# DeltaNet stage of a one-core layer: another interleaving of steps, inverses and dense units

## The chip, the core and the metric

The kernel runs on one core of a Trainium2 chip. A core has five engines with a queue of instructions each: PE (TensorE, matrix products into PSUM), DVE (VectorE), ACT (ScalarE), POOL (GpSimd) and SP (SyncE, here only for transfers). Each engine takes its instructions in order, and semaphores make one wait for another. DMA transfers are issued from the queues of SP, ACT and POOL. The metric is the device time of one execution in microseconds (us).

## The reference, cut to what matters

One layer over 640 tokens (128 of context, 512 latent), 1024 wide, in float32. The input is normalised and modulated, and projected to queries, keys and values of an attention branch, to those of a gated DeltaNet branch, and to gates. The outputs of both branches are projected, gated, added and projected again; a feed-forward part follows. The change touches the DeltaNet branch and what runs beside it:

```python
def _gated_delta_chunked(q, k, v, g, beta, s0):      # chunks of 64 tokens, 8 heads of 64
    ...
    a_mat = jnp.where(strict, einsum('nbhid,nbhjd->nbhij', kbeta, kb) * decay, 0.0) + jnp.eye(CHUNK)
    sol = lax.linalg.triangular_solve(a_mat, rhs, left_side=True, lower=True, unit_diagonal=True)
    qk = einsum('nbhid,nbhjd->nbhij', qb, kb) * decay
    def step(S, xs):
        v_new = uc - einsum('bhck,bhkv->bhcv', wc, S)
        o = einsum('bhck,bhkv->bhcv', qc * exp(gcc), S) + einsum('bhij,bhjv->bhiv', qkc, v_new)
        S = S * exp(glast) + einsum('bhck,bhcv->bhkv', kc * exp(glast - gcc), v_new)
        return S, o
```

It runs once forward and once backward over the tokens; for each direction the context gives a state of its own, and the latent tokens start from a given state. The chunks of one direction depend on each other through S.

## The kernel before, in words

The kernel goes through these stages: normalising and modulating the input; the DeltaNet projections and their convolution; the DeltaNet stage, in which the other projections ("dense units") run beside the recurrence; the attention; the merge; the feed-forward part. The change is in the DeltaNet stage, with small edits ahead of it and behind it.

**Dense units.** `dense(kinds)` walks over a string of letters and yields after each unit. `v`: the values of the attention, 5 units of 24 matmuls; `q`: a block of its queries or keys, 2 units of 24; `g`: a block of gates, 2 units of 24; `m` and `a`: a column block of the modulation weights, 1 unit of 16 matmuls, with a few more behind the next unit. The list that runs beside the recurrence is `FILL[1] = "vqmqmqmqmqmqmqmgmgagagagagagagaggagggggg"`: 67 units, with an `m` or an `a` after each pair of `q` or `g` for most of its length. A unit's weights are loaded raw on SP's queue into one of two buffers (`load_raw`, tag `raw`), and split into two float32r parts, `whi` by ACT (line 177) and `wlo` by DVE (line 178); three products (lines 197 to 199) make up one float32 product. `m` and `a` use raw weights (line 226). The result goes through ACT into a buffer of tag `gth` (three of them, shared with the rows of `m` and `a` and with the small gate tiles `gbn`) and is stored to DRAM on SP's queue (lines 879, 892, 904).

**Inverses.** `prep(mf, mb, buf)` prepares a pair of token tiles, one for each direction, in the order of `PAIRS` (five pairs, two steps of 64 tokens in each). It is a generator; its parts are: loads of decay logarithms into `rls` on POOL's queue (638, 639) and of stored gram matrices; three decay tiles (matmuls 603, 604 into the PSUM tile `ps_tb`, then an exp on ACT, 606) with the gram matrices (623) and their products `U` and `KQD`; then a substitution of 15 rounds on DVE (687 to 690) and a transpose `Zp` (698); then four small products, each depending on the one before by way of ACT or DVE: line 706 to `Gm` (ACT, 709), line 714 to `Yp` and `Zq` (DVE, 716 and 718), line 726 to `Gm` (731), lines 737 and 739 to `YZ` (748, 749). Lines 706 and 714 are 128 matmuls each.

**Steps.** `step` is a generator of three parts: (0) matmuls of the keys and queries with the state S (783), `kS` and `r` on DVE (786, 787); (1) `YZ` times `r` (793), then `vd` and `vn` on DVE (796, 798), `qS` and the scaled state on ACT (802, 808), and for a tile's second visit the load of the earlier output and its sum with `qS` on POOL (814); (2) `vd` into the new state (822, added on DVE at 825) and `vn` into the output (834). The right-hand side `r` is loaded on POOL's queue one step ahead (760). After a second visit `finish_o` normalises the output: a square on ACT (850, tile `fz`), a sum on DVE (852), a Newton iteration, a product on POOL (860) with a z tile loaded on ACT's queue (859), and four slots later a transpose on PE (598) and a store to `od_d` (868).

**The order.** PE's instructions stand in the order in which the program writes them (`manual_schedule`). The program is written in *slots*: `slot(*parts)` writes the next part of each generator given, then a part of each open `finish_o`, then one dense unit. The other engines' order comes from a planner that takes what is ready by its model, highest priority first; the priority says in how many slots a part is due. So between two parts in neighbouring slots lies one dense unit on PE. Before the change a step's parts stand in neighbouring slots, and so do the inverse's last four parts: 14 slots ahead of the first step, then for each pair the three slots of each of its two steps (two for the very first), one slot with a part of the inverse after next, four with the last four parts of the next inverse (the first two of which hold parts of the inverse after next as well), and five slots at the end. That is 67 slots.

The attention stage starts with loads of `qk_d` on ACT's queue (1057), rotations on DVE and POOL (1059 to 1070) and score matmuls (1084). Its filler on PE are the products of the merge's DeltaNet half, which read `od_d` (1156, 1157). `issue_after(ins)` puts the instructions that a block writes for the engine of `ins` behind `ins` in that engine's order; it adds nothing on other engines.

Of the kernel before, what the change touches and what calls it, by code (L numbers as in the profile page):

```python
# [18 lines left out]
P = 128  # L19
# [78 lines left out]
def body(ctx: ExitStack, tc: tile.TileContext, I, O, dbg=None):  # L98
# [64 lines left out]
    rawp = [None, 0]  # L163

    def load_raw(src, pool=None, tag="raw"):
# [108 lines left out]
    xa = tk.tile([P, 5, 512], F32, tag="xa", name="xa")  # L274
# [30 lines left out]
    with tc.tile_pool(name="xp", bufs=1, side="right") as xp:  # L305
# [4 lines left out]
        xTs = [y.rearrange("p t c -> p (t c)").rearrange("p (k c) -> p k c", k=4) for y in (xa, kt)]  # L310
        xT = [y[:, k] for y in xTs for k in range(4)]
        rawp[:] = [xp, 6]
        with tc.manual_schedule(engines={mybir.EngineType.SP}):
# [4 lines left out]
            for a, b in ((0, 2), (2, 4), (4, 5)):  # L318
# [8 lines left out]
                for t in range(a, b):  # L327
                    for i in range(2):
                        V.tensor_scalar(xh[i][:, t], xh[i][:, t], rr[:, t - a : t - a + 1], None, op0=ALU.mult)
                        ps = ps_t3()  # L330
                        for q in range(4):
                            PE.transpose(ps[:, q * 128 : q * 128 + 128], xh[i][:, t, q * 128 : q * 128 + 128], ident)
                        (S.copy if i == 0 else V.tensor_copy)(xTs[i][:, :, t * 128 : t * 128 + 128], ps.rearrange("p (k c) -> p k c", k=4))
# [142 lines left out]
    rls = tk.tile([P, 2, 640], F32R, tag="xa", name="rls")  # L476
# [102 lines left out]

    YZb = [[dn.tile([P, 512], F32, tag=f"YZ{d}{i}", name=f"YZ{d}{i}") for i in range(2)] for d in range(2)]  # L580
# [50 lines left out]
    def prep(mf, mb, buf):  # L631
# [13 lines left out]
        for d, m in ((0, mf), (1, mb)):  # L645
# [23 lines left out]
            kq = dn.tile([P, 512], F32, tag="KQD", name=f"KQD{d}", bufs=4)  # L669
# [31 lines left out]
        pg_ = ps_st(0)  # L701
# [9 lines left out]
        pc_ = ps_st(2)  # L711
# [9 lines left out]
        pg2 = ps_st(0)  # L721
# [11 lines left out]
        pc2 = ps_st(1)  # L733
# [7 lines left out]
        YZ = [YZb[d][buf] for d in range(2)]  # L741
# [8 lines left out]
        prs.append(dict(YZ=YZ, KQD=KQD, m=(mf, mb)))  # L750
# [12 lines left out]
    def step(si, pr, r, st, first, last=False):  # L763


        m = pr["m"]
# [9 lines left out]
        if St is not None:  # L776
# [10 lines left out]
            hold[:] = [V.tensor_tensor(r, r, kS, op=ALU.subtract).ins]  # L787
            yield
        pv = ps_st(1)
# [57 lines left out]
    def finish_o(ot, hv, rq, rq2):  # L847

        fz = dn.tile([P, 512], F32, tag="fz", name="fz")
# [21 lines left out]
    def fill_v(c):  # L871
        w = load_tok(I["w_v"][c], 256)
        cs = slice(c * 256, c * 256 + 256)
        for t in range(5):
# [4 lines left out]
            nc.sync.dma_start(v_d[t, :, cs], vv[:, :256])  # L879
            if t == 0:  # L880
                nc.sync.dma_start(O["vc"][:, cs], vv[:, :256])
            yield

    def fill_qk(i):
        hp, mi = i // 2, i % 2
        whi, wlo = load_w(I["w_qk"][i], KT, 128)
        for half in range(2):
# [4 lines left out]
            nc.sync.dma_start(qk_d[hp, mi, :, half * 320 : half * 320 + 320], vv)  # L892
            if mi == 1 and half == 0:
                nc.sync.dma_start(O["kc"][hp], vv[:, 0:128])
            yield

    def fill_gate(j):
        whi, wlo = load_w(I["w_gate"][j], KT, 128)
        for half in range(2):
# [4 lines left out]
            nc.sync.dma_start(gt_d[j, :, half * 320 : half * 320 + 320], th)  # L904
# [28 lines left out]
    hold = []  # L933
# [15 lines left out]
    with tc.manual_schedule(engines={mybir.EngineType.PE}):  # L949
# [13 lines left out]
        preps = [prep(*PAIRS[n], n % 2) for n in range(5)]  # L963
# [11 lines left out]
        for n in range(5):  # L975
            P1, P2 = [preps[i] if i < 5 else iter(()) for i in (n + 1, n + 2)]
            ahead(5, P2)
# [17 lines left out]
            if n < 3:  # L995
                slot((1, P2))
            if n < 4:
                for i in range(4):
                    slot((1, P1), *([((1, 8)[i], P2)] if i < 2 else []))
            if n == 3:  # L1000
                dpx.close()
        for _ in range(5):
# [20 lines left out]
    with (  # L1023
# [596 lines left out]
```

## Time and profile before

| | |
|---|---|
| median of 3 runs | 1173.38 us (1173.02 to 1174.58) |
| profiled execution | 1170.73 us, its span 1168.9 us |
| PE busy over the span | 1083.1 us (93%) |
| DVE, ACT, POOL busy | 861.3, 523.7, 342.3 us |
| granted clock, mean | 0.970 |

The span runs from the first to the last instruction; the time of an execution is a little longer. Busy time of PE counts matmuls in flight, so a busy PE isn't one at its peak. The granted clock is the share of its full rate that PE was given. Waits are put down to what ended last before the waiting instruction ran; "issue" is time for which the profile shows no cause. A DMA or a wait of a queue's sequencer has a q behind the engine's name.

### The profile page before, as it was taken

The numbers are of one execution on the slowest core, as the hardware profiler recorded it, in microseconds if no ns is written. First come the engines' busy times: TensorE is split into PE (matmuls) and PEld (weight loads), VectorE is DVE, ScalarE is ACT, GpSimd is POOL, SyncE is SP. The second block draws the span as 40 slices with busy tenths as digits, with TensorE's granted clock in tenths as the row PEclk, the third lists the DMA queues.
The fourth block names the chain that finished last, engine by engine and source line by source line (L and its number), as shares of the span: only waits on it lengthen the run. The fifth ranks groups of instructions, "written<-read, shape, count | busy, mean of one in ns | idle before, by whom it ended". The sixth has DMA issues, their size and how long they took to land.

```text
span 1168.9 us, 25017 instructions
## 1 busy us (share of the span) xinstructions
PE 1083.1 (93%) x10016; PEld 959.6 (82%) x10016; DVE 861.3 (74%) x1676; ACT 523.7 (45%) x1133; POOL 342.3 (29%) x277
## 2 busy tenths in 40 slices
PE   4999999989898988978999999979999999999996
PEld 3779999888787777876777899978979898897975
DVE  6567896884758486564755767887897989889785
ACT  5436343535453533424435353545544444444532
POOL 1343312101000001321221415544453544435213
PEclk9999999999999998987999999989999999999999
DMA  8831015656654534734333662066654565665515
GB/s 304 311 120 45 22 38 189 227 185 172 206 174 143 172 124 130 217 118 135 95 112 106 218 253 91 36 175 159 181 153 129 143 164 147 175 171 152 165 36 145
DMA packets 74421, 176.39 MB, mean 151 GB/s; under 512 B 16952, under 2 KB 31048, under 8 KB 74304
## 3 DMA queue, kind: packets, MB, share of 16 engines
q1 hardware_dynamic: 42416, 119.92, 30.5%
q10 hardware_dynamic: 26000, 37.16, 10.2%
q0 software_dynamic: 5888, 17.71, 8.2%
q8 instruction: 79, 1.29, 0.4%
q14 instruction: 38, 0.31, 0.1%
HBM read 150.63 MB, written 24.12 MB: 150 GB/s over the span
## 4 chain that ended last, share of the span: by engine, by line
PE 56%; DVE 10%; DMA 6%; ACT 3%; issue 2%; ACTq 1%; POOL 0%; DVEq 0%; SPq 0%; POOLq 0%
PE ps_mm L197 6%; PE ps_mm L198 6%; PE ps_mm L199 6%; DVE wlo L178 4%; PE ps_mm L1317 3%; PE ps_mm L1315 3%; PE ps_mm L1316 3%; PE ps_st L1316 2%; PE ps_st L1315 2%; PE ps_st L1317 2%; DVE R L1405 2%; DMA od_d<-oT 1%; PE ps_tp L1423 1%; PE ps_tp L1424 1%; PE ps_tp L1422 1%
## 5 line engine op out<-in xcount | busy, mean ns | idle before, releaser
L197 PE MATMUL ps_mm<-hhi,whi 128*128 128x320 f32 x576 | 189.2, 329 | 0.6 <-ACT qk L891 0.6
L198 PE MATMUL ps_mm<-hlo,whi 128*128 128x320 f32 x576 | 183.6, 319 | 4.3 <-issue 4.3
L199 PE MATMUL ps_mm<-hhi,wlo 128*128 128x320 f32 x576 | 182.6, 317 | 0.0
L178 DVE TENSOR_TENSOR wlo<-raw,whi 128x1024 fp32r<-128x1024 f32 x94 | 122.5, 1309 | 54.5 <-ACT whi L177 50.9
L177 ACT CAST whi<-raw 128x1024 fp32r<-128x1024 f32 x117 | 121.5, 1045 | 88.1 <-PE ps_mm L198 47.8
L198 PEld LDWEIGHTS ps_mm<-hlo,whi 128*128 128x128 f32 x576 | 112.9, 196 | 4.9 <-issue 4.8
L197 PEld LDWEIGHTS ps_mm<-hhi,whi 128*128 128x128 f32 x576 | 112.8, 196 | 4.7 <-ACT qk L891 1.1
L199 PEld LDWEIGHTS ps_mm<-hhi,wlo 128*128 128x128 f32 x576 | 112.6, 196 | 0.0
L178 POOL TENSOR_TENSOR wlo<-raw,whi 128x1024 fp32r<-128x1024 f32 x23 | 56.2, 2449 | 87.7 <-ACT whi L177 87.7
L178 DVE TENSOR_TENSOR wlo<-S,whi 128x1024 fp32r<-128x1024 f32 x28 | 55.4, 2003 | 6.4 <-ACT whi L177 6.4
L760 POOL DMA_DIRECT2D r<-vs_d x20 | 10.8, 543 | 164.5 <-PE ps_st L793 149.5
L178 DVE TENSOR_TENSOR wlo<-T,whi 128x1024 fp32r<-128x1024 f32 x28 | 44.0, 1573 | 16.8 <-ACT whi L177 16.8
L514 DVE SCALAR_TENSOR_TENSOR y<-cvb,cw,y 128x644 f32<-128x644 f32 x48 | 45.4, 946 | 1.0
L177 ACT CAST whi<-T 128x1024 fp32r<-128x1024 f32 x28 | 29.4, 1049 | 34.4 <-PE ps_mm L1316 17.7
L1100 POOL TENSOR_SCALAR bias<-bias 128x256 f32<-128x256 f32 x24 | 22.1, 935 | 72.2 <-DMA bias<-in_bias_dram 69.8
L177 ACT CAST whi<-S 128x1024 fp32r<-128x1024 f32 x28 | 28.6, 1051 | 29.3 <-PE ps_tb L199 10.9
L1317 PE MATMUL ps_mm<-mhi,wlo 128*128 128x320 f32 x112 | 34.0, 312 | 1.3 <-DVE wlo L178 1.2
L1315 PE MATMUL ps_st<-mhi,whi 128*128 128x320 f32 x112 | 34.5, 308 | 0.0
L1316 PE MATMUL ps_st<-mlo,whi 128*128 128x320 f32 x112 | 34.5, 308 | 0.0
L1317 PE MATMUL ps_st<-mhi,wlo 128*128 128x320 f32 x112 | 34.5, 308 | 0.0
L1315 PE MATMUL ps_mm<-mhi,whi 128*128 128x320 f32 x112 | 34.4, 308 | 0.0
L1316 PE MATMUL ps_mm<-mlo,whi 128*128 128x320 f32 x112 | 34.4, 308 | 0.0
(539 smaller groups left out, 3326.9 us busy)
## 6 DMA issues: line engine op xcount, KB each, us to landing
raw<-in_w_ff_dram SPq DMA_DIRECT2D x57, 512.0 KB
raw<-in_w_ada_dram SPq DMA_DIRECT2D x48, 512.0 KB
raw<-in_w_gate_dram SPq DMA_DIRECT2D x16, 512.0 KB
S<-in_w_ff_dram SPq DMA_DIRECT2D x14, 512.0 KB
S<-in_w_ff_dram POOLq DMA_DIRECT2D x14, 512.0 KB, 5.9
T<-in_w_ff_dram SPq DMA_DIRECT2D x14, 512.0 KB
T<-in_w_ff_dram POOLq DMA_DIRECT2D x14, 512.0 KB, 7.2
raw<-in_w_dn_dram SPq DMA_DIRECT2D x12, 512.0 KB
```

The costliest lines, as they stand in the source:

```text
L177: S.copy(hi, raw)
L178: eng.tensor_tensor(lo, raw, hi.bitcast(F32), op=ALU.subtract)
L197: PE.matmul(out, ah, bh, start=(i == 0), stop=False)
L198: PE.matmul(out, ah, bl, start=False, stop=False)
L199: PE.matmul(out, al, bh, start=False, stop=(i == n - 1))
L514: V.scalar_tensor_tensor(y, b[:, j : j + 644], cw[:, mt * 5 + j : mt * 5 + j + 1], y, op0=ALU.mult, op1=ALU.add)
L1100: G.tensor_scalar(bt[:, 0:256], bt[:, 0:256], -1.0, None, op0=ALU.mult)
L1315: PE.matmul(o, hi[:, k, fs], bh, start=(first and k == 0), stop=False, skip_group_check=not first)
L1316: PE.matmul(o, hi[:, k, fs], bl, start=False, stop=False, skip_group_check=not first)
L1317: PE.matmul(o, lo[:, k, fs], bh, start=False, stop=(k == 3), skip_group_check=not first)
L1405: V.tensor_tensor(dst, dst, ps, op=ALU.add)
L1422: PE.matmul(ps[pair], ah, w[0][:, k], start=(first and k == 0), stop=False, skip_group_check=not first)
```

## The change

- The slots are written anew. A step's parts stand two slots apart, and so do the last four parts of the inverse; a step and an inverse take turns. Inside a pair, part 2 of the first step and part 0 of the second stand in neighbouring slots. The inverse has one part more (the split is behind the substitution), and part 8 of an inverse stands beside part 0 of its own pair's first step; `step` therefore looks up its inverse only in part 1. With 12 slots ahead of the first step, 11 for each pair (10 for the fourth) and 5 at the end there are 71 slots for the same 67 units.
- The inverse's four products go to the PSUM tiles `ps_tb` and `ps_tp` instead of the steps' `ps_st`.
- `KQD` has three sets: two in `dn`, and a third in the second half of the former tile `xa`, which is split in two tiles; the copies that fill it at the start of the kernel become two each for the first half of the input.
- While the slots run, every third raw weight goes to a buffer of its own (`raw3`).
- The stores of the `v`, `q` and `g` units move from SP's queue to POOL's.
- `fz` takes the buffer of `kS` instead of one of its own.
- `hold` keeps the last step's lines 787 (DVE) and 814 (POOL), and everything that the first attention pair writes up to its rotated keys is put behind them; before, the block held only the loads, which are on ACT's queue.

```diff
     def load_raw(src, pool=None, tag="raw"):
+        if raw3[0] and tag == "raw":
+            raw3[1] += 1
+            if raw3[1] % 3 == 0:
+                pool, tag = (raw3[0], 1), "raw3"
...
-                        (S.copy if i == 0 else V.tensor_copy)(xTs[i][:, :, t * 128 : t * 128 + 128], ...)
+                        if i == 0:
+                            for j in range(2):
+                                S.copy(xa[j][:, :, t * 128 : t * 128 + 128], pk[:, 2 * j : 2 * j + 2])
...
+    kx = tk.tile([P, 2, 640], F32, tag="xa1", name="kx")
+    KQb = [[dn.tile([P, 512], F32, tag=f"KQ{d}{i}", name=f"KQ{d}{i}") for d in range(2)] for i in range(2)]
+    KQb.append([kx.rearrange("p a c -> p (a c)")[:, 512 * d : 512 * d + 512] for d in range(2)])
...
-            kq = dn.tile([P, 512], F32, tag="KQD", name=f"KQD{d}", bufs=4)
+            kq = KQb[buf % 3][d]
...
             V.tensor_tensor(Y[:, q:, :], Y[:, q:, :], tq[:, q:, :], op=ALU.subtract)
+        yield
...
-        pg_ = ps_st(0)
+        pg_ = ps_tb()
...
-        pc_ = ps_st(2)
+        pc_ = ps_tp()
...
-        pg2 = ps_st(0)
+        pg2 = ps_tb()
...
-        pc2 = ps_st(1)
+        pc2 = ps_tp()
...
-            hold[:] = [V.tensor_tensor(r, r, kS, op=ALU.subtract).ins]
+            hold[0] = V.tensor_tensor(r, r, kS, op=ALU.subtract).ins
             yield
+        pr = prs[n]
...
-                G.tensor_tensor(ot, ot, qS, op=ALU.add)
+                hold[1] = G.tensor_tensor(ot, ot, qS, op=ALU.add).ins
...
-        fz = dn.tile([P, 512], F32, tag="fz", name="fz")
+        fz = dn.tile([P, 512], F32, tag="kS", name="fz")
...
-            nc.sync.dma_start(gt_d[j, :, half * 320 : half * 320 + 320], th)
+            nc.gpsimd.dma_start(gt_d[j, :, half * 320 : half * 320 + 320], th)
...
+        raw3[0] = dn
         for n in (0, 1):
             ahead(1, preps[n])
-            for _ in range(3):
-                slot((5, preps[n]))
-        for _ in range(4):
+            for i in range(3):
+                slot(((1, 1, 8)[i], preps[n]))
+            if n == 0:
+                ahead(5, preps[n])
+        for _ in range(3):
             slot()
-        for _ in range(4):
+        for _ in range(3):
             slot((1, preps[0]))
...
-            for a in range(2):
-                si = 2 * n + a
-                s_ = step(si, prs[n], r, st, (a == 0) if n == 0 else n <= 2, si == 9)
-                for i in range(0 if st[0] is not None else 1, 3):
-                    slot((1, s_))
-                    if i == 1 and si < 9:
-                        with due(2):
-                            r = rhs(si + 1, PAIRS[(si + 1) // 2])
+            P0, P1, P2 = [preps[i] if i < 5 else none for i in (n, n + 1, n + 2)]
+            s_ = step(2 * n, n, r, st, n <= 2)
+            if n == 0:
+                slot((1, P0))
+            else:
+                slot((1, s_), (1, P0))
+            ahead(2, P2)
+            ahead(6, P1)
+            slot((1, P2))
+            slot((1, s_))
+            with due(3):
+                r = rhs(2 * n + 1, PAIRS[n])
+            if n != 3:
+                slot((1, P2))
+            slot((1, s_), (8, P2))
+            s_ = step(2 * n + 1, n, r, st, 0 < n <= 2, n == 4)
+            slot((1, s_))
+            slot((1, P1))
+            slot((1, s_))
+            if n < 4:
+                with due(3):
+                    r = rhs(2 * n + 2, PAIRS[n + 1])
+            slot((1, P1))
+            slot((1, s_))
+            slot((1, P1))
...
-            if n < 3:
-                slot((1, P2))
-            if n < 4:
-                for i in range(4):
-                    slot((1, P1), *([((1, 8)[i], P2)] if i < 2 else []))
...
+            rx = ExitStack()
+            if hp == 0:
+                for ins in hold:
+                    rx.enter_context(tc.issue_after(ins))
             for mi in range(2):
-                with tc.issue_after(hold[0]):
-                    nc.scalar.dma_start(x, qk_d[hp, mi])
+                nc.scalar.dma_start(x, qk_d[hp, mi])
...
+            rx.close()
```

The stores of lines 879, 881, 892 and 894 change as the one of line 904 does.

More of the change, by code (lines that the diff above doesn't have):

```diff
@@ L273, in body @@
     kt = tk.tile([P, 5, 512], F32, tag="kt", name="kt")
-    xa = tk.tile([P, 5, 512], F32, tag="xa", name="xa")
+    xa = [tk.tile([P, 2, 640], F32, tag=f"xa{i}", name=f"xa{i}") for i in range(2)]
     beta = tk.tile([P, 5, 16], F32, tag="beta", name="beta")
@@ L309, in body @@
               for i in range(2)]
-        xTs = [y.rearrange("p t c -> p (t c)").rearrange("p (k c) -> p k c", k=4) for y in (xa, kt)]
-        xT = [y[:, k] for y in xTs for k in range(4)]
+        xT1 = kt.rearrange("p t c -> p (t c)").rearrange("p (k c) -> p k c", k=4)
+        xT = [xa[k // 2][:, k % 2] for k in range(4)] + [xT1[:, k] for k in range(4)]
         rawp[:] = [xp, 6]
@@ L475, in body @@
             nc.sync.dma_start(aj_d[5 * d : 5 * d + 5, i].rearrange("m h t -> h m t"), neg)
-    rls = tk.tile([P, 2, 640], F32R, tag="xa", name="rls")
+    rls = tk.tile([P, 2, 640], F32R, tag="xa0", name="rls")
     rls = [rls[0:32, d] for d in range(2)]
@@ L740, in prep @@
                           tile_position=(64 * par + 32, 64 * par + 32))
-        YZ = [YZb[d][buf] for d in range(2)]
+        YZ = [YZb[d][buf % 2] for d in range(2)]
         for qd in range(4):
@@ L749, in prep @@
             S.activation(h8(YZ[1])[r2, :, 0:32], pc2[r2, :256].rearrange("p (h c) -> p h c", h=8), AF.Copy, scale=-1.0)
-        prs.append(dict(YZ=YZ, KQD=KQD, m=(mf, mb)))
+        prs.append(dict(YZ=YZ, KQD=KQD))
     def halves(si, m):
@@ L761, in rhs, with step @@
         return r
-    def step(si, pr, r, st, first, last=False):
-        m = pr["m"]
+    def step(si, n, r, st, first, last=False):
+        m = PAIRS[n]
         St = st[0]
@@ L878, in fill_v @@
             S.copy(vv[:, :256], ps[:, :256])
-            nc.sync.dma_start(v_d[t, :, cs], vv[:, :256])
+            nc.gpsimd.dma_start(v_d[t, :, cs], vv[:, :256])
             if t == 0:
-                nc.sync.dma_start(O["vc"][:, cs], vv[:, :256])
+                nc.gpsimd.dma_start(O["vc"][:, cs], vv[:, :256])
             yield
@@ L891, in fill_qk @@
             S.activation(vv, ps[:, :320], AF.Copy, scale=(-0.125 if mi == 0 else 1.0))
-            nc.sync.dma_start(qk_d[hp, mi, :, half * 320 : half * 320 + 320], vv)
+            nc.gpsimd.dma_start(qk_d[hp, mi, :, half * 320 : half * 320 + 320], vv)
             if mi == 1 and half == 0:
-                nc.sync.dma_start(O["kc"][hp], vv[:, 0:128])
+                nc.gpsimd.dma_start(O["kc"][hp], vv[:, 0:128])
             yield
@@ L931, in body @@
     prs, fin = [], []
-    hold = []
+    hold = [None, None]
     now = [0]
@@ L961, in slot @@
             now[0] += 1
-        preps = [prep(*PAIRS[n], n % 2) for n in range(5)]
+        preps = [prep(*PAIRS[n], n) for n in range(5)]
+        none = iter(())
+        raw3[0] = dn
         for n in (0, 1):
             ahead(1, preps[n])
-            for _ in range(3):
-                slot((5, preps[n]))
-        for _ in range(4):
+            for i in range(3):
[3 more added lines that the diff above has]
+        for _ in range(3):
             slot()
-        for _ in range(4):
+        for _ in range(3):
             slot((1, preps[0]))
```

8 lines of the change are left out of this document (5 added, 3 removed).

## The prediction

> **What bounds the kernel now.** I read the busy times by stage first, since the share over the whole span (PE 93%) hides where TensorE stands still. The columns are the stretch, its length, then busy time of PE, weight load, DVE, ACT, POOL, the granted clock and the DMA share.
>
> ```profile
> 229.00:518.00 289.00, 252.89 (x4778) 225.76 (x4778) 196.24 (x578) 123.22 (x343) 35.95 (x43) 0.94 0.52 165
> ```
>
> From 229 to 518 us run the DeltaNet steps, the inverses and the dense units between them. PE is idle for 289.0 - 252.9 = 36.1 us there, and the mean clock is 0.94. DVE, the next busiest, has 93 us free, so no engine other than PE bounds this stage by its work. Who PE waited for in that stretch (total, times, longest):
>
> ```profile
> PE ps_st L793 <- issue: 11.6, 3, 6.3
> PE ps_st L822 <- DVE vd L796: 6.3, 3, 4.9
> PE ps_mm L198 <- issue: 4.3, 1, 4.3
> PE ps_st L726 <- DVE Zq L718: 3.1, 1, 3.1
> PE ps_st L714 <- issue: 3.0, 3, 2.0
> PE ps_st L793 <- DVE r L787: 2.5, 1, 2.5
> PE ps_st L783 <- DVE S L825: 2.1, 1, 2.1
> PE ps_tb L603 <- ACT Dm L606: 1.3, 1, 1.3
> PE ps_st L793 <- ACT YZ L749: 1.2, 1, 1.2
> ```
>
> These nine rows make 35.4 of the 36.1 us. No row names the raw weights: the list is short waits of one part of a step, or of the inverse, for the DVE or ACT work behind the part before it. The idle time also costs clock. Stretches that run at half clock, two of seven and their sum:
>
> ```profile
> 382.80:386.20 3.40, 3.40 (x47) 3.28 (x38) 1.48 (x4) 3.06 (x14) 0.00 (x0) 0.50 0.89 231
> ...
> 444.20:451.00 6.80, 5.90 (x47) 5.82 (x48) 4.53 (x9) 2.71 (x10) 3.40 (x4) 0.50 0.35 117
> ...
> sum 34.00, PE 30.56 PEld 30.12 DVE 25.86 ACT 14.38 POOL 7.23; mean PE 4.37 PEld 4.30 DVE 3.69 ACT 2.06 POOL 1.03
> ```
>
> PE was busy 30.56 us at half clock, work of 15.3 us at full clock, so 15.3 us more are lost: 0.42 us for each idle one. The stage could give back 36.1 + 15.3 = 51.4 us, no more.
>
> How long one dense unit covers a part is in PE's order around one step:
>
> ```profile
> 327.17 1.16 PE L783 MATMUL ps_st<-S,kqS 64*64 64x64 f32 x64
> 331.97 1.15 PE L793 MATMUL ps_st<-r,YZ 64*64 64x64 f32 x32
> 333.05 1.07 PE L226 MATMUL ps_mm<-raw,csl 128*32 128x256 f32 x16
> 334.98 0.81 PE L822 MATMUL ps_st<-vd,kt 64*64 64x64 f32 x32 [0.86 <-DVE vd L796]
> ```
>
> Between L783 and L793 lies a long unit (24 matmuls, `q` or `g`): 331.97 - 328.33 = 3.6 us, and no wait. Between L793 and L822 lies a short one (`m` or `a`, L226): 1.07 us, and PE waits. The list has a short unit after every two long ones, so about every third part has 1.07 us of cover.
>
> **Part by part. Two units apart.** Two neighbours in the list hold at least one long unit, so a gap of two covers at least 3.6 + 1.07 = 4.7 us.
>
> The r chain (L793, 11.6 + 2.5 = 14.1 us, four waits) gets 3.6 us more in each. Three of them are shorter than that, at most 6.3 - 3.6 = 2.7 us of the longest is left, and that one stood among the attention's rotary work on DVE, which the new `issue_after` puts behind the last step's L787. I take 0. YZ (1.2) and Dm (1.3): 0 as well.
>
> The longest wait for vd (4.9) is not latency. The chain of waits shows it:
>
> ```profile
> 303.52 11.01 DMA od_d<-oT
> ...
> 314.63 2.26 DMA fzt<-z_d
> 316.90 1.23 DVE wlo L178
> 318.13 0.61 DVE vd L796
> ```
>
> ACT's queue stood at the z load until a store of 11 us had landed; `whi` and `wlo` were late behind it, and `vd` stands behind `wlo` on DVE. Nothing in the change removes that; the added cover leaves 4.9 - 3.6 = 1.3 us. The other two vd waits vanish.
>
> The chain from L822 over S to the next L783 still has one unit inside each pair. It needs 381.87 - 377.84 = 4.0 us:
>
> ```profile
> 377.15 0.69 PE L822 MATMUL ps_st<-vd,kt 64*64 64x64 f32 x32
> ...
> 381.87 1.86 PE L783 MATMUL ps_st<-S,kqS 64*64 64x64 f32 x64 [2.09 <-DVE S L825]
> ```
>
> I counted the new slots against the list: only in the first pair is that unit short, and there decay and grams matmuls stand beside it. 0.
>
> The inverse: L706 to L714 to L726, and what stands between them now:
>
> ```profile
> 346.93 1.07 PE L226 MATMUL ps_mm<-raw,csl 128*32 128x256 f32 x16
> ...
> 348.72 1.21 PE L714 MATMUL ps_st<-Yp,Gm 32*32 32x32 f32 x119 [0.51 <-issue]
> ```
> ```profile
> 401.16 1.29 PE L706 MATMUL ps_st<-Zp,U 16*32 16x32 f32 x128
> ...
> 406.63 1.29 PE L714 MATMUL ps_st<-Yp,Gm 32*32 32x32 f32 x128
> ...
> 408.58 1.07 PE L226 MATMUL ps_mm<-raw,csl 128*32 128x256 f32 x16
> 412.77 1.44 PE L726 MATMUL ps_st<-Zq,U 32*32 32x32 f32 x64 [3.12 <-DVE Zq L718]
> ```
>
> L714 stalls inside its own group ("issue": nothing waited for) with a short unit ahead, and runs through with a long one (from 401 on). I put the 4.3 us of L198, which also waited for nothing the profile shows, to the same cause: two bursts of 128 tiny matmuls close together. Now every two bursts have a long unit between them. Of 3.0 + 4.3 = 7.3 us between 0 and all remain; I take 1.0, by the unbroken row. Zq needs 412.77 - 407.92 = 4.9 us from the end of L714; the first inverse still has a single short unit there (slot 11 of the new order), so 4.9 - 1.1 = 3.8 remain, which I take; the later ones have two units.
>
> **What it adds.** *Stores on GpSimd's queue.* SP loses its waits for ACT, but those never reached PE. POOL gets them:
>
> ```profile
> SPq L904 <- ACT gth L903: 75.5, 19, 8.4
> ```
> ```profile
> POOL rls L638 <- PE ps_tb L603: 27.5, 4, 8.1
> POOL fzt L860 <- DVE foy L856: 25.9, 4, 12.0
> ```
> ```profile
> L760 POOL DMA_DIRECT2D r<-vs_d x16: 516/530/749, 257.4 to 449.2; - x16
> ...
> DMA to landing us min/median/max: 2.4/3.7/6.4
> ```
>
> A store costs POOL 0.53 us (the r load's row); one for each of the 51 `v`, `q` and `g` units of the list is 27 us on an engine busy 36 of 289, and that is covered. What counts is the order. Behind a store that waits for ACT stand r, rls, L814 and L860, each with two units of slack; behind a waiting rls or L860 stand stores, and on a store waits the ring of three `gth` buffers, hence ACT's next result, hence PE once both ps_mm buffers are full. That takes two long units, 7.3 us. Only the longest wait, 12.0, is beyond: 12.0 - 7.3 = 4.7 us, which I take; the lower bound is 0, the upper one the second rival below.
>
> *fz in kS's buffer.* Now L786 must wait for L852, in the four steps that follow a finishing one. DVE waited for ACT's square, 4.8 us in three of the five:
>
> ```profile
> L850 ACT ACTIVATE fz<-ot x5: 612/627/634, 279.7 to 513.6; 128x512 f32<-128x512 f32 x5
> ...
>   ACT fz L850: 4.8, 3
> ```
>
> Between 0 and 4.8 us; half, 2.4. *Third raw buffer, third key set, the inverse's PSUM tiles moved to tp and tb*: no row shows PE waiting for raw weights or KQD, so no gain of their own. They allow the new order; tb has one buffer, freed by an exp, and the cost if its cover went would be the row of L603, 1.3 us. *xa in two tiles*: five more ACT copies,
>
> ```profile
> L333 ACT COPY xa<-ps_tp x3: 585/586/589, 14.5 to 20.6; 128x512 f32<-128x512 f32 x3
> ...
>   DVE mod L240: 8.3, 3
> ```
>
> at most 5 x 0.59 = 2.9 us, beside 8.3 us for which ACT waits there anyway: 0.
>
> *The end.* The new order has 71 slots for 67 units, so the last transposes (L598) come after the last unit, where two units followed before.
>
> ```profile
> 526.39 0.60 PE L598 MATMUL ps_tp<-cst,ot 128*128 128x128 f32 x4
> ...
> 548.94 0.90 PE L197 MATMUL ps_mm<-doh,whi 128*128 128x384 f32 x2 [1.38 <-ACT doh L1157]
> ```
>
> The filler of the attention starts 22.5 us after L598, so it starts about two units (7.3 us) later against the attention. The attention runs meanwhile: 0 to 7.3, I take 2.
>
> **Sum.** Idle left: 1.3 (vd) + 1.0 (bursts) + 3.8 (Zq) + 4.7 (stores) + 2.4 (fz) = 13.2 us, times 1.42 for the clock 18.7. Gain 51.4 - 18.7 - 2 = 30.7 us. The profiled execution took 1170.7 (span 1168.9), the median is 1173.4, 2.7 above: 1140.0 by the one, 1142.7 by the other. DVE's 196 us would fill 77% of a stage of 289 - 51.4 + 18.7 = 256 us, so it does not become the bound.
>
> On the clock, the Trainium skill (TensorE: Matmul & The Clock Gate, Part 1: The HAM clock gate) says that PE drops to half after an idle window of about 3.4 us. The trace agrees on the half and on the steps of 3.4 us, but shows 382.8 to 386.2 at half after a wait of 2.1 us. By that rule only the longest waits (6.3, 4.9, 4.3 and the like) would cost clock, and the gain would be up to 5 us less (three stretches of 3.4 us at half).
>
> **The rivals.** *Half the gain.* The wait for vd (4.9) and the three r waits of the first row (11.6) come from the order in which ACT and DVE take their work, not from latency, and return elsewhere: 16.5 us idle, times 1.42, is 23.4, less the 1.3 x 1.42 counted already: 21.6, so 1164. For it: the 11 us store shows how far ahead of its data a queue can stand. Against: two units swallow all but the longest.
>
> *Slower: stores late on POOL.* Place: the eight `a` units, where `adarow`, `gbn` and `gth` share the ring. A store behind a POOL wait of 6.5 us (25.9 / 4), plus 0.5 issue, 3.7 landing and 0.6 on ACT (L850's row), is done 11.3 us after its unit; beyond 7.3 PE stands still, 4.0 x 8 x 1.42 = 45 us: 1188. It decides from a landing 7.3 us after the unit's end. Against: POOL idles most of the stage. The Trainium skill speaks for this rival (SBUF — State Buffer, "SBUF: two separate sides"): DMAs issued from GpSimd starve while DVE holds the port they share, 3.1 us in place of 0.62. The r load's 0.52 to 0.75 us, with DVE busy 68%, does not show it.
>
> *It does not do what it says:* every gap is of the order, and each one removed comes back in another place, as 51.4 us are shared among all: 1173. For it: no wait names a weight, a key set or a store, the things it changes. *More:* only bursts and the first inverse stay, (1.0 + 3.8) x 1.42 = 6.8: 1173.4 - 44.6 = 1129.
>
> **How the numbers follow.** Forecast, 1131 to 1154: 46%. More gain: 8%. Half: 25%. No change, within 0.2% (2.3 us, about what the measurement can tell): 6%. Slower: 15%. Faster is 46 + 8 + 25 = 79%. The range leaves out the slower case and part of the largest gain: 1126 to 1171.
>
> **What would show it.** Right: idle PE of about 13 us in the DeltaNet stage and two or three half-clock stretches; the rows of r, Zq, S and YZ gone; L714 unbroken. Wrong: waits of L793 for r behind kS (fz), ACT's `gth` waiting for DMAs of GpSimd's queue, `whi` late, or 25 us and more of idle PE in that stage.

## The result

The change made the kernel slightly slower: 1180.44 us in the median of 9 runs (1172.01 to 1182.44) against 1173.3 of before, a ratio of 1.0055 with a 95% interval of 1.003 to 1.0081. The forecast was 1142.7 us, the range 1126 to 1171; the time lies above it. A ratio here compares undisturbed runs of a kernel and of the kernel before on the same chip, so it isn't the quotient of the two medians.

The profiled execution of the changed kernel took 1181.05 us (span 1179.3). Figures of a stage, here and below, are of one execution of each kernel; the times of the nine runs lie some 10 us apart. The view of busy times by stretch shows the DeltaNet stage and the attention, with the columns explained ahead of the prediction:

```profile
229.00:522.00 293.00, 261.32 (x4829) 233.54 (x4828) 191.86 (x562) 124.79 (x346) 59.54 (x86) 0.92 0.50 161
522.00:655.00 133.00, 119.61 (x725) 93.76 (x724) 74.01 (x232) 55.63 (x157) 27.00 (x29) 0.87 0.36 114
```

The attention before, for the second row:

```profile
518.00:644.00 126.00, 120.24 (x765) 94.53 (x764) 66.77 (x211) 56.71 (x159) 23.47 (x24) 0.93 0.37 116
```

PE still idles 293.0 - 261.32 = 31.7 us in the stage, where the prediction had expected some 13 after the change, and the clock is lower, not higher (0.92 for 0.94). The attention's clock fell from 0.93 to 0.87.

For PE, the list of waits of that stretch after the change (total, times, longest; L202 is L197 of before, L740 is L726, L751 is L737, L720 is L706, L797 is L783, L808 is L793, L837 is L822):

```profile
PE ps_mm L202 <- ACT gth L918: 8.9, 6, 5.6
PE ps_mm L202 <- ACT qk L906: 6.7, 2, 6.4
PE ps_tp L751 <- ACT Gm L745: 3.8, 4, 1.7
PE ps_tb L740 <- DVE Zq L732: 3.8, 1, 3.8
PE ps_tb L720 <- DVE Zp L712: 1.9, 1, 1.9
PE ps_st L808 <- ACT YZ L762: 1.6, 1, 1.6
...
PE ps_tb L720 <- issue: 1.0, 1, 1.0
```

The waits of before for r (14.1 us), vd (6.3), S (2.1) and Dm (1.3) are gone. The wait for YZ isn't: 1.2 us before, 1.6 here and 0.8 in a row of L808 for L763. In place of what went, PE waits 15.6 us for something that had cost it 0.6 us before (L197 for `qk`): the two PSUM buffers of the dense units (`ps_mm`), which ACT's `gth` and `qk` copies free.

The half-clock stretches of the stage, two of seven and their sum:

```profile
285.88:296.12 10.24, 4.14 (x15) 4.14 (x16) 8.28 (x36) 2.75 (x10) 2.39 (x3) 0.50 0.69 211
...
364.38:374.62 10.24, 6.20 (x23) 6.20 (x24) 3.07 (x9) 2.48 (x7) 0.54 (x1) 0.50 0.29 94
...
sum 44.38, PE 32.58 PEld 32.29 DVE 29.80 ACT 16.92 POOL 6.67; mean PE 4.65 PEld 4.61 DVE 4.26 ACT 2.42 POOL 0.95
```

**Where the 10.4 us of span came from.** The stage is measured here in every profile from the start of PE's first `m` unit (229.02 us before, 229.47 after) to the start of the last matmul of the last unit: 305.52 us before, 302.85 after, so 2.7 us were won. The attention's first score matmul starts 4.1 us ahead of that end before and 2.3 behind it after (6.4 lost), the attention then takes 114.9 us in place of 110.4 (4.5 lost), and all that lies ahead of the stage and behind the attention loses 2.2. The stage gave almost nothing, and its end gave away more than that.

### The profile page after: what moved, and what is told of

Same layout as the page of the kernel before. It is cut to its first block, busy times and chain, and to the rows that moved or that the text cites. A ratio compares the mean times of both kernels' runs of the same rounds, so it can differ in the third digit from the quotient of the medians.

```text
span 1179.3 us, 25049 instructions
## 1 busy us (share of the span) xinstructions
PE 1089.8 (92%) x10016; PEld 965.5 (82%) x10016; DVE 861.9 (73%) x1676; ACT 524.0 (44%) x1138; POOL 377.6 (32%) x341
## 4 chain that ended last, share of the span: by engine, by line
PE 60%; DVE 20%; DMA 8%; ACT 5%; issue 4%; ACTq 2%; POOL 1%; DVEq 0%; SPq 0%; POOLq 0%
PE ps_mm L202 7%; PE ps_mm L203 6%; PE ps_mm L204 6%; DVE wlo L183 4%; PE ps_mm L1352 3%; PE ps_mm L1350 3%; PE ps_mm L1351 3%; DVE y L524 2%; DVE R L1440 2%; PE ps_st L1351 2%; PE ps_st L1350 2%; PE ps_st L1352 2%; DVE y L522 1%; ACT whi L182 1%; PE ps_st L1148 1%
## 5 line engine op out<-in xcount | busy, mean ns | idle before, releaser
L202 PE MATMUL ps_mm<-hhi,whi 128*128 128x320 f32 x576 | 191.0, 332 | 17.4 <-ACT gth L918 10.7
L202 PEld LDWEIGHTS ps_mm<-hhi,whi 128*128 128x128 f32 x576 | 114.2, 198 | 21.7 <-ACT gth L918 12.1
L919 POOL DMA_DIRECT2D gt_d<-gth x32 | 17.9, 560 | 122.2 <-ACT gth L918 111.6
L524 DVE SCALAR_TENSOR_TENSOR y<-cvb,cw,y 128x644 f32<-128x644 f32 x48 | 42.8, 892 | 1.0
```

Source lines behind the costliest of these rows:

```text
L202: PE.matmul(out, ah, bh, start=(i == 0), stop=False)
L524: V.scalar_tensor_tensor(y, b[:, j : j + 644], cw[:, mt * 5 + j : mt * 5 + j + 1], y, op0=ALU.mult, op1=ALU.add)
L919: nc.gpsimd.dma_start(gt_d[j, :, half * 320 : half * 320 + 320], th)
```

## The experiments

Each edit is made on the changed kernel unless it says otherwise.

**e1: the units' stores back on SP's queue.**

```diff
-            nc.gpsimd.dma_start(gt_d[j, :, half * 320 : half * 320 + 320], th)
+            nc.sync.dma_start(gt_d[j, :, half * 320 : half * 320 + 320], th)
```

> The changed kernel with the stores of the v, q and g units back on SP's queue. If stores late on GpSimd's queue hold the gth ring (my second rival), the waits of the dense units for ACT's gth and qk, 17.4 us in the profile of the changed kernel, mostly go, and with their clock the time falls by 15 to 25 us, to about 1160. If ACT drains the units late because its own queue stands in order behind waits for DVE and for DMAs, those waits stay at 12 to 20 us and the time stays within 0.4% of the changed kernel's.

1192.23 us, ratio 1.0175 (1.0136 to 1.0213): 1.2% slower than the changed kernel, which neither expectation had. (The 17.4 us of the expectation are counted from 204 to 560 us, the 15.6 above from 229 to 522.) The stores on GpSimd's queue are a gain in the changed kernel; the slower rival, by which they would come late there, falls. They do wait long on POOL, and in this stage a single wait of 1.0 us (DVE's, for `gbn`) is put down to one of them (waits of POOL in the changed kernel, then landing times of these stores):

```profile
POOL gt_d L919 <- ACT gth L918: 106.9, 20, 12.8
POOL qk_d L907 <- ACT qk L906: 48.2, 8, 12.1
```
```profile
L919 POOL DMA_DIRECT2D gt_d<-gth x32: 539/559/610, 334.4 to 534.2; - x32
...
DMA to landing us min/median/max: 2.0/2.5/6.3
```

**e6: the kernel before, with only these stores on GpSimd's queue.**

> The kernel before with nothing changed but the stores of the v, q and g units, on GpSimd's queue. If SP's in-order queue holds back the raw weights in either order, it falls by 5 to 14 us, as the new order does. If, as the profile of before says, no wait for weights reaches PE in the old order, it stays within 0.3%, and the 12 us that the stores are worth in the new order are a need of that order.

1172.27 us, 1.0008 (0.9988 to 1.0029): no change. By itself the move does nothing for the kernel before.

**e2: the eight loads of `vw` at the start of the attention on SP's queue in place of ACT's.** They stand on ACT's queue behind the last store to `od_d`, which now comes after the last unit. ACT's part of the timeline of the changed kernel (start, duration, the idle time before it in brackets):

```profile
535.33 0.92 ACTq L883 DMA_DIRECT2D od_d<-oT  x2
536.29 7.79 ACTq L1061 DMA_DIRECT2D vw<-v_d  x8
544.13 0.61 ACT L1143 ACTIVATE pr<-s,st 128x384 f32<-128x384 f32 x1 [8.83 <-DMA vw<-v_d]
```

```diff
-                    nc.scalar.dma_start(vw[:, b, kt], ...)
+                    nc.sync.dma_start(vw[:, b, kt], ...)
```

> The changed kernel with the eight loads of vw at the start of the attention on SP's queue instead of ACT's. If these loads, 7.8 us on ACT's queue between the last store of od_d and the first exp, hold up the attention, the two waits of the scores for the row minimum (1.5 and 5.4 us) go and the time falls by 5 to 9 us, to 1171 to 1175. If the late end of the last finishing part alone costs the time, it falls by 2 us at most.

1176.22 us, 1.0021 (0.9993 to 1.0049), by the ratios 0.34% or 4 us less than the changed kernel, with intervals that overlap. The attention takes 107.6 us in place of 114.9. The first exponential waited 8.83 us for loads that it does not use, and most of that was ACT issuing: the eight loads take 0.52 to 1.66 us each there, 7.6 us together, and 0.50 to 0.66 us each on SP's queue in e2. Not all of the 7.3 us is what the change had lost: the attention of before took 110.4, and there too ACT issues the eight loads ahead of its first exponential (its timeline before the change):

```profile
530.55 3.37 ACTq L1031 DMA_DIRECT2D vw<-v_d  x5
...
534.89 3.30 ACTq L1031 DMA_DIRECT2D vw<-v_d  x3
538.23 0.61 ACT L1108 ACTIVATE pr<-s,st 128x384 f32<-128x384 f32 x1 [2.91 <-DMA vw<-v_d]
```

That exponential comes 7.8 us after the first score matmul (530.44 us); it is 9.5 us in the changed kernel and 3.5 in e2.

**e3: the loads and stores of the steps, the finish and the inverses on SP's queue in place of ACT's.** The two longest waits of PE in this stage of the changed kernel, in ACT's and PE's timeline:

```profile
286.24 0.60 ACTq L1028 DMA_DIRECT2D S<-in_state_dram  x1
...
289.01 0.63 ACTq L1028 DMA_DIRECT2D S<-in_state_dram  x1
...
291.49 0.44 ACT L906 ACTIVATE qk<-ps_mm 128x320 f32<-128x320 f32 x1 [2.83 <-DMA S<-in_state_dram]
```
```profile
291.98 0.64 PE L202 MATMUL ps_mm<-hhi,whi 128*128 128x320 f32 x1 [6.39 <-ACT qk L906]
```
```profile
366.70 1.11 ACTq L858 DMA_DIRECT2D o_d<-ot  x2
367.93 0.44 ACT L918 ACTIVATE gth<-ps_mm 128x320 f32<-128x320 f32 x1 [2.67 <-DVE gbn L255]
```
```profile
368.42 0.64 PE L202 MATMUL ps_mm<-hhi,whi 128*128 128x320 f32 x1 [5.58 <-ACT gth L918]
```

ACT takes its work in order. Transfers that wait or are being issued, and DVE's late small gate tiles, hold the copies that empty `ps_mm`, and PE stands until they run. In the second case both end close together: DVE's L255 at 367.52 us, the issue of the second store at 367.81.

```diff
-                nc.scalar.dma_start(ot[sl], o_d[mm, sl])
+                nc.sync.dma_start(ot[sl], o_d[mm, sl])
...
-                        nc.scalar.dma_start(st[0][hs, d], si_[hq, :, d])
+                        nc.sync.dma_start(st[0][hs, d], si_[hq, :, d])
```

Likewise lines 656, 679, 858, 874, 883 and 1024.

> The changed kernel with the DMAs of the steps, the finishing parts and the inverses (o_d, ot, z, od_d, gst, gr_d, S) on SP's queue instead of ACT's. If ACT drains the dense units late because it stands at its own DMAs, the 17.4 us of waits for gth and qk fall below 9 and the time by 8 to 15 us. If it stands behind DVE's backlog, the waits stay above 12 us; raw weights behind waiting stores on SP can then even make it up to 10 us slower.

1172.78 us, 1.0 (0.9978 to 1.0023), 0.55% less than the changed kernel. The waits for `gth` and `qk` fall from 15.6 to 11.5 us, the one for `Gm` (L751) rises from 3.8 to 6.4, and the stage takes 294.9. So ACT's standing at transfers is part of it, not all. That DVE makes the rest isn't shown.

**e5: e2 and e3 together.**

> The changed kernel with both moves: the loads of vw and the DMAs of steps, finishing parts and inverses on SP's queue. If they are two costs at two places (the start of the attention and the dense units' drain), their gains add up: 1180 - 4 - 8, 1168 +- 3, with the attention's part near 108 us and the last dense unit near 525 us. If both only free the same ACT time, it stays at 1172 or above.

1167.22 us, 0.9954 (0.993 to 0.9978). The two add up, as far as the intervals tell.

**e4: without the third raw buffer; e8: that, and `fz` in a buffer of its own; e7: without the rule on the first attention pair.**

```diff
-        raw3[0] = dn
```
```diff
-        fz = dn.tile([P, 512], F32, tag="kS", name="fz")
+        fz = dn.tile([P, 512], F32, tag="fz", name="fz")
```
```diff
-            if hp == 0:
-                for ins in hold:
-                    rx.enter_context(tc.issue_after(ins))
```

> The changed kernel without the third raw weight buffer. By the prediction the buffer gains nothing of its own: the time stays within 0.3%. If weights had become the tight spot in the new order, PE waits for whi or wlo appear and the time rises by 5 us or more.

> The changed kernel without the third raw buffer and with fz in a buffer of its own again (compare with the run without the third raw buffer). If the wait of kS for the finishing square costs what I predicted, 2.4 us idle with its clock, it is 3 to 4 us faster than that run; if it is hidden, within 2 us of it.

> The changed kernel without the rule that puts the first attention pair's rotations behind the last step. If the rule keeps DVE free for the last r, as I predicted, PE waits for r again in the last steps and the time rises by 3 to 8 us. If the rule makes the attention late, the attention starts nearer to the last dense unit and the time falls by 3 to 6 us.

1.0086 (1.0052 to 1.012), 1.0072 (1.0048 to 1.0095) and 1.0058 (1.0033 to 1.0083), against 1.0055 of the whole change: none of the three moves the time by more than the intervals tell. The times of e4 and e8 are known to 3 or 4 us each and can't settle the 2.4 us taken for `fz`; but no wait of PE for `r` stands in the lists of the changed kernel, of e4 or of e8, so nothing of it reached PE.

**e9: the copies of `Zq` into `YZ` on DVE in place of ACT; e10 and e11: e5 with these copies on DVE and on POOL.**

```diff
-            S.copy(h8(YZ[1])[QD[qd], :, c0 : c0 + 32], Zp[QD[qd], 8:16])
+            V.tensor_copy(h8(YZ[1])[QD[qd], :, c0 : c0 + 32], Zp[QD[qd], 8:16])
```

> The changed kernel with the copies of Zq into YZ on DVE instead of ACT. In the profile of the changed kernel ACT stands 18.7 us in front of these copies for DVE's Zq, with finished dense units behind it. If that is what holds the ps_mm buffers, PE's waits for gth and qk fall from 17.4 to below 10 us and the time by 5 to 12 us. If ACT is late for other reasons, it stays within 3 us, or rises by DVE's extra 6 us of copies.

> The kernel with vw and the steps' DMAs on SP's queue (1167.2 us), and the Zq copies on DVE. If ACT's stand at Zq (25.6 us there) is the next thing in line, it falls by 4 to 10 us, to 1157 to 1163. If not, within 3 us.

> The same with the Zq copies on GpSimd. It takes the wait to a queue where stores stand behind it. If any queue but ACT's will do, it is within 2 us of the one with the copies on DVE; if stores behind the copies fill the ring of gth, it is 3 us or more slower than that one.

1.0104 (1.0067 to 1.0141), 0.9969 (0.9945 to 0.9994) and 0.9979 (0.9954 to 1.0003): no gain anywhere. ACT does stand at these copies in the changed kernel (its list of waits):

```profile
ACT YZ L759 <- DVE Zq L732: 18.7, 4, 7.1
```

But taking them off ACT brings no time. PE's waits for `gth` and `qk` stay at 15.1 us in e9; in e10 they fall from e5's 12.3 to 8.7, and the time doesn't follow.

**e12: the kernel before, its old order, with all moves of queues: the units' stores on GpSimd's, e2's and e3's on SP's.**

> The kernel before, in its old order, with the same three moves: unit stores on GpSimd's queue, vw and the DMAs of steps, finishing parts and inverses on SP's. If ACT's queue is what the moves free whatever the order, it falls by 4 to 9 us as the new order did, and the new order itself is worth nothing or less. If the gain needs the new order, it stays within 3 us of the kernel before.

1158.89 us, 0.9899 (0.9865 to 0.9933): the lowest ratio of this study. What the changed kernel adds to e12 beside the moves (e5, 0.9954) costs 0.55%. The next six runs ask which part does.

**e15: the kernel before with e3's moves alone.**

> The kernel before, with only the loads and stores of the steps, the finish and the inverses moved from ACT's queue to SP's; vw's loads stay on ACT's, the units' stores on SP's. Theory: ACT's standing at these transfers cost the kernel before as it cost the changed one (8 us in e3), so 1163 to 1167, ratio 0.991 to 0.995, and the stores on GpSimd's queue (no gain alone in e6) and vw bring the rest of e12's 14.5 us. Rival: on SP's queue these transfers stand behind the units' stores, which wait for ACT, so that the raw weights come late, as in e1: no gain, 1172 or more, and the moves pay only together.

1170.17 us, 0.9989 (0.9967 to 1.0011): nothing that can be told. Its stage is 4.1 us shorter, its attention 2.4 longer (112.8 us, 104.4 in e12). The expectation of 0.991 to 0.995 was wrong; alone, neither this move nor e6's pays in the old order. Which of the remaining two, `vw`'s loads or the units' stores, makes the rest of e12's gain wasn't tried.

**e13: e5 with the slots written as before the change** (and without the part more that the inverse has), so the old order with all other edits.

```diff
-            if n == 0:
-                slot((1, P0))
-            else:
-                slot((1, s_), (1, P0))
...
+            for a in range(2):
+                si = 2 * n + a
+                s_ = step(si, n, r, st, (a == 0) if n == 0 else n <= 2, si == 9)
+                for i in range(0 if st[0] is not None else 1, 3):
+                    slot((1, s_))
```

> All edits of the change and the moves of e5 (the loads and stores of the steps, the finish and the inverses, and the loads of vw, on SP's queue; the stores of the units on GpSimd's), but the slots written as before the change, so that the steps' parts and the inverse's stand one dense unit apart again. If the new order of the slots is what costs 8 us between e12 (1158.9) and e5 (1167.2): about 1159, ratio 0.988 to 0.992. If the other edits cost it (the inverse's PSUM tiles tb and tp, the third key set, the third raw buffer, fz in kS's buffer, the rule on the attention's first pair): about 1167, ratio 0.995. Half each would be 1163.

1174.83 us, 1.0021 (0.9996 to 1.0045): outside of both theories. The other edits cost the old order 1.2%, and the new slots win 0.7% of it back.

**e14: e5 with the last pair's steps one unit apart** (67 slots for 67 units).

```diff
-            if n != 3:
+            if n < 3:
                 slot((1, P2))
...
-            slot((1, P1))
-            slot((1, s_))
+            if n < 4:
+                slot((1, P1))
+            slot((1, s_))
```

The pair's other two slots with a part of `P1` go in the same way.

> e5 with the last pair of steps (which stands beside no inverse) one dense unit apart, as before the change: four slots fewer, 67 slots for 67 units, so that the last transposes and the store of od come before the last units again. If the late end of the steps is what the new order costs: 1160 to 1163, since e5's attention starts 2.9 us behind the last unit's end and takes 109.0 us, and e12's starts 4.1 us ahead of it and takes 104.4. If the waits among the steps cost it: 1166 to 1168, for the last pair's own waits for r and vd come back, up to 3 us, against a handover no worse than e5's.

1165.9 us, 0.9959 (0.9937 to 0.9981), which the intervals can't tell from e5. In its profile the attention starts 0.2 us behind the last unit in place of 2.9 and takes 105.6 us in place of 109.0. Against that, the stage takes 1.4 us more, and it begins 3.9 us later (230.54 us for 226.63), which the edit doesn't explain. So the late end is not seen to cost e5 time; by the two intervals up to some 3 us may be hidden.

**e16: e12 with the inverse's products in `ps_tb` and `ps_tp`; e17: e13 with them back in `ps_st`; e18: e5 with them back in `ps_st`.** The edit of e16; the other two are its inverse:

```diff
-        pg_ = ps_st(0)
+        pg_ = ps_tb()
...
-        pc_ = ps_st(2)
+        pc_ = ps_tp()
...
-        pg2 = ps_st(0)
+        pg2 = ps_tb()
...
-        pc2 = ps_st(1)
+        pc2 = ps_tp()
```

> e12 (the order of before, the moves of the queues) with one edit of the change more: the inverse's four products in the PSUM tiles tb and tp in place of the steps' st. Theory: the one buffer of tb, shared with the decay matmuls of the next inverse, and tp, shared with the grams and the transposes, cost what lies between e12 (0.990) and e13 (1.002): ratio 0.998 to 1.003, with waits of L603 for Gm as in e13 (3.7 us). Rival: the cost is in the other edits (key sets, third raw buffer, fz in kS's buffer, the rule on the attention's first pair): 0.988 to 0.993.

> e13 (old slots, all other edits, the moves of the queues) with the inverse's products back in the tiles st. If PSUM is what e13 lost against e12: 0.988 to 0.993. If the other edits are: 0.998 to 1.003. With e16 the two must add up to e13's loss, or the edits depend on each other.

> e5 (new slots, all edits, the moves of the queues) with the inverse's products back in the tiles st. If the PSUM tiles cost the same in the new order, the waits of L720 and L751 (1.6 + 2.8 + 6.9 us in e5) shrink and the ratio falls from 0.995 to 0.985 to 0.990, under e12's. Rival: in the new order a step and an inverse take turns, so that st is held by both and PE waits for it: no gain or a loss, 0.995 to 1.005, with new waits for st tiles.

1172.13, 1162.87 and 1176.14 us. All six kernels with the queues moved, by order and by the inverse's PSUM tiles:

| | inverse in st | inverse in tb and tp |
|---|---|---|
| old slots | e12 0.9899 (0.9865 to 0.9933) | e16 0.9999 (0.9979 to 1.002) |
| old slots, other edits | e17 0.9906 (0.9878 to 0.9935) | e13 1.0021 (0.9996 to 1.0045) |
| new slots, other edits | e18 1.0017 (1.0003 to 1.0031) | e5 0.9954 (0.993 to 0.9978) |

The four lines that move the inverse to tb and tp cost the old order 1.0 to 1.15%, 12 to 13 us; the other edits cost it nothing. The new slots alone cost 1.1% too (e17 to e18). Both together cost 0.5% (e17 to e5), close to what the whole change costs without the moves (0.55%). Each of the two makes the other bearable, and neither is a gain over the old order.

PE's waits in e18 show why the new slots need other tiles than st. A step now finds the inverse's result in its tile, and the inverse the step's:

```profile
PE ps_st L797 <- ACT Gm L745: 6.9, 2, 6.5
PE ps_st L720 <- ACT qS L817: 6.2, 3, 3.9
PE ps_st L837 <- DVE Yp L730: 5.5, 3, 2.5
...
PE ps_st L740 <- DVE S L840: 3.7, 1, 3.7
```

And e16, against e12, shows what tb costs in the old order: the decay matmuls of the next inverse (L603) wait for `Gm` of this one in the one buffer of tb, and L706 for `Dm`. PE's waits of e16, then its stage and that of e12:

```profile
PE ps_tb L603 <- ACT Gm L709: 3.7, 3, 2.3
...
PE ps_tb L706 <- ACT Dm L606: 2.0, 1, 2.0
```
```profile
229.00:518.00 289.00, 251.65 (x4713) 224.09 (x4711) 190.68 (x555) 121.02 (x338) 59.47 (x82) 0.91 0.50 160
```
```profile
229.00:518.00 289.00, 258.60 (x4835) 232.08 (x4832) 196.49 (x577) 126.65 (x350) 63.43 (x89) 0.96 0.53 168
```

PE idles 6.9 us more there in e16 (258.60 - 251.65); the two waits for tb, which have no match of their size in e12, are 5.7 us. The clock is 0.91 there and 0.96 in e12.

## Why the prediction was wrong

**What held: the arithmetic of the stage.** Idle time, and half of PE's busy time at half clock, make up most of what changes in this stage. The stage's length less both lies between 251.1 and 254.1 us in all twenty profiles, six of which are (rounded one by one):

| | stage, us | idle | lost at half clock | rest |
|---|---|---|---|---|
| before | 305.5 | 36.1 | 15.4 | 254.0 |
| after | 302.9 | 33.4 | 16.3 | 253.1 |
| e5 | 298.1 | 31.9 | 14.2 | 252.0 |
| e12 | 296.4 | 30.4 | 11.9 | 254.1 |
| e16 | 314.4 | 37.7 | 23.4 | 253.3 |
| e18 | 304.1 | 33.0 | 20.0 | 251.1 |

So 51.4 us could be given back, as the prediction had it. Of these, 49.7 were there after the change.

**The step that failed: 51.4 less what is left of the old waits.** The sum counted what would remain of each wait of before, added something for stores and `fz`, and took every other wait as 0. It didn't ask what PE would wait for next. It put the idle time left at 13.2 us, and 33.4 were measured. All waits counted as gone did go but YZ's, and the size of two left-overs was right: Zq of the first inverse, taken at 3.8, measured 3.76 (the prediction's list of signs had its row as gone), and the bursts, taken at 1.0, 1.0. The second is in part luck: the stall now stands inside L720, and no longer inside L728 (L714 of before).

```profile
244.54 1.14 PE L231 MATMUL ps_mm<-raw,csl 128*32 128x256 f32 x16
249.45 1.77 PE L740 MATMUL ps_tb<-Zq,U 32*32 32x32 f32 x59 [3.76 <-DVE Zq L732]
```

But PE now runs ahead of ACT until both `ps_mm` buffers are full, and stands there for `gth` and `qk`. The prediction weighed this ring only for late stores; what was late was ACT itself: behind transfers on its own queue, as e3 shows for 4.1 of the 15.6 us, and behind DVE, as the timeline has it and no run shows. The wait for `Gm` (L751), 0.2 us before at L737, takes 3.8. The prediction's chain of waits had shown such a stand of ACT (11 us at the z load), and it was set down as one event of 4.9 us. The rival of half the gain (25%, 1164 us) named this mechanism and was too small: nearly all of the idle time came back, as in the rival "it does not do what it says" (6%, 1173).

**PSUM tiles taken at 0.** "tb has one buffer, freed by an exp, and the cost if its cover went would be the row of L603, 1.3 us": in the old order it costs about 12 us (e16 against e12), of which that row has 3.7. By the arithmetic above, e16's stage idles 7.3 us more than e12's and loses 11.5 more at half clock; the same four lines between e17 and e13 make 6.1 and 6.7. In the changed kernel's list no wait of PE for tb behind another part shows, and in the new order tb and tp are better than st by 0.6% (e5 against e18), so there the move is the price of the order and not a loss beside it. A term at nothing needs the list of who else uses the buffer: here the decay matmuls, the grams and the transposes.

**The handover, taken at 2 of 0 to 7.3 us.** The start of the attention moved by 6.4 us, within the bounds. That the attention itself would take 4.5 us more was not in them. PE idles 9.0 us of it in place of 4.1: before, the last unit ran on PE (to 534.8 us) while ACT issued the eight loads (530.55 to 538.18); after, the units end at 532.6 and the loads begin at 536.29. The prediction followed PE's filler, and not the queue on which the next stage begins.

**Stores and `fz`.** 4.7 us for the stores had the wrong sign: they are a gain in the changed kernel (e1) and nothing in the one before (e6). Of the 2.4 us for `fz` no wait of PE shows anything (e4, e8). The chance of 15% for slower was placed on the stores; slower came by other ways.

**The clock.** 0.42 us lost for each idle one was the mean of before. After the change it is 16.3 / 33.4 = 0.49, in e12 11.9 / 30.4 = 0.39 and in e16 23.4 / 37.7 = 0.62. A stretch at half clock doesn't need a long wait ahead of it: the two of 10.24 us begin 0.3 and 1.5 us after the waits of 6.39 and 5.58 us begin, and in the 3.41 us ahead of each of the changed kernel's seven PE was busy for 0.77 to 2.25 us. The Trainium skill (TensorE: Matmul & The Clock Gate, Part 1: The HAM clock gate) has PE fall to half after an idle window of about 3.4 us; the trace does not agree, as none of the seven windows was idle throughout.

**What stays open.** Why the new order with tb and tp is still 0.5% behind the old with st is not settled to a single wait: e5 has 1.7 us more in the stage than e12, an attention 4.6 us longer (granted clock over it 0.89 for 0.97) that starts 7.0 us later against the last unit, and e14, which mends the late start, wins nothing. By which path the stores on SP's queue cost e1 its 1.2% is open too: PE's waits for `gth` and `qk` are 15.8 us there, as without the edit, and its stage is 9.3 us longer. That a shorter ACT chain for `gth` alone, or a third `ps_mm` buffer, would bring the gain wasn't tried.

## What to carry to other kernels

When waits are covered by moving parts apart, price what the waiting engine runs into next: the buffers it fills ahead and the in-order engine that empties them, with every transfer queued on that engine. A transfer keeps the engine that issues it (ACT for 8.83 us at `vw`'s loads), and so belongs on the queue of an engine with nothing else to do; moving transfers off ACT and the stores off SP brought 1.0% with no change of the order (e12), and the new order was no gain over it. A PSUM tile that is moved is priced by who else uses the new one.

## What the runs showed that was not expected

- The same stores moved to GpSimd's queue are worth 1.2% in the changed kernel (e1) and nothing in the one before (e6), at 0.56 us of issue each.
- Moves of transfers of which two alone bring nothing that can be told (e6, e15) bring 1.0% together and with `vw`'s (e12). The Trainium skill (Trainium Kernel Development and Optimization, Key Constraints) says that issuing from several engines only saves issue time. At `vw`'s loads that is what costs: 7.6 of the 8.83 us for which ACT stood are issues. Ahead of `qk`'s copy at 291.49 us ACT stood 2.83 us, and two issues make up 1.0 of them.
- With 7.3 us more of idle PE, in waits of at most 3.1 us, went 11.5 us more lost at half clock (e16 against e12): more than the waits themselves. Between e17 and e13 it is 6.7 for 6.1.
